# Last eight blocks of a row-mean laid out so that a partition ends with sixteen neighbouring rows, stored as 128 runs of 64 B

## Chip, cores and metric

One core of one Trainium2 chip. The metric is the device time of one execution in microseconds; the median of several executions is quoted.

The *span* runs from the program's first instruction to its last one. The *time* is longer by what is called *outside* below. SyncE *issues* the transfers; the issue is the time that it spends on handing one over. Each load raises a semaphore by 16, in single counts (the records of the kernel before have 176 for eleven loads); a store is waited for at 16 too, in fewer records for the small ones (5 for the last store of the kernel before). The *landing* of a transfer is when its last count arrives.

## The reference

```python
x = np.random.randn(64, 256, 8192).astype(np.float32)   # 512 MiB

def reference(x):
    return np.mean(x, axis=2)                             # (64, 256) float32
```

That is 16384 rows of 8192 numbers, each row one mean.

## The kernel before

The 16384 rows are 64 blocks of 256 rows: 128 partitions (`P`) times two rows (`R`). Loads of 8 MiB go through three slots; VectorE sums them. The last block comes in shrinking pieces, shared between VectorE and ScalarE, so that little work is left when the last byte lands.

```python
    NB = N // (P * R)          # 64 blocks
    LB = NB - 1                # the last block is treated apart
    x_v = x_f[0 : LB * P * R].rearrange("(p n r) s -> n p r s", p=P, r=R)
    x_l = x_f[LB * P * R : N].rearrange("(r p) s -> r p s", p=P)
    out_bulk = o_f[0 : LB * P * R].rearrange("(p n) -> p n", p=P)
    out_last = o_f[LB * P * R : N].rearrange("(r q j) -> r q j", q=P // SQ, j=SQ)
    # ... cut ...
    def store_last(r):         # a column of 128 sums -> 4 rows of 32 sums -> 4 runs of 128 B
        nc.vector.transpose(out=fin_t[r][:], in_=fin[r][:])
        return nc.sync.dma_start(out=out_last[r], in_=fin_t[r][0:P:SQ, :])
    # ... 63 loads and sums, the chunks of the last block: cut ...
    nc.vector.tensor_scalar_mul(out=bulk[:], in0=res[:], scalar1=inv)
    nc.sync.dma_start(out=out_bulk, in_=bulk[:])
    scaled_sum(fin[0][:, 0:1], head[:])
    st = store_last(0)
    # ... cut ...
    untracked(scaled_sum(fin[1][:, 0:1], fin_in[:, 0 : lastw + k]))._wait_ge(sem, 16)
    with tc.issue_after(st.ins):
        last_store = store_last(1)
```

In the bulk each partition owns 126 neighbouring rows of HBM, so partitions lie 4032 KiB apart. In the last block neighbouring rows lie in neighbouring partitions, and each column of 128 sums must be turned before it can be stored in long runs. The kernel also writes its own exit. There GpSimd clears the semaphores and then waits for the last store:

```python
    with nc.body("clears", parent=parent, valid_engines=[POOL]):
        nc.gpsimd.sem_clear(range(used[0], stored))
        nc.gpsimd.wait_ge(last_sem, 16).then_inc(last_sem, -16)
```

Of the kernel before, what the change touches and what calls it, by code (L numbers as in the profile page):

```python
# [8 lines left out]
SLOTS = 3  # L9
LOAD_SEMS = 6  # L10
FETCH_BLOCK = 128
LAST_CHUNKS = (4096, 2048, 1024, 512, 256, 256)

ACT_FROM = 512
SQ = 32


@with_exitstack
def kernel(
# [5 lines left out]
    nc = tc.nc  # L25
    P = nc.NUM_PARTITIONS
    F32 = mybir.dt.float32
# [4 lines left out]
    B, C, S = x.shape  # L32
    N = B * C
    R = ROWS
    assert R == 2 and N % (P * R) == 0, (N, P, R)
    NB = N // (P * R)
    LB = NB - 1
    assert SLOTS <= LB and sum(LAST_CHUNKS) == S
    inv = 1.0 / float(S)
    half = S // 2  # L40

    x_f = x.rearrange("b c s -> (b c) s")
    o_f = out.rearrange("b c -> (b c)")

    x_v = x_f[0 : LB * P * R].rearrange("(p n r) s -> n p r s", p=P, r=R)
    x_l = x_f[LB * P * R : N].rearrange("(r p) s -> r p s", p=P)
    out_bulk = o_f[0 : LB * P * R].rearrange("(p n) -> p n", p=P)
    out_last = o_f[LB * P * R : N].rearrange("(r q j) -> r q j", q=P // SQ, j=SQ)

    pool = ctx.enter_context(tc.tile_pool(name="sb", bufs=1))  # L50
    slots = [nc.alloc_sbuf_tensor(f"xt{i}", [P, R, S], F32) for i in range(SLOTS)]
    load_sem = [tc.alloc_semaphore(f"load{i}") for i in range(LOAD_SEMS)]
    tail_sem = [tc.alloc_semaphore(f"tail{i}") for i in range(len(LAST_CHUNKS) + 1)]

    res = pool.tile([P, LB * R], F32)
    bulk = pool.tile([P, LB * R], F32)
    fin = [pool.tile([P, SQ], F32, name=f"fin{r}") for r in range(R)]
    fin_t = [pool.tile([P, SQ], F32, name=f"fin_t{r}") for r in range(R)]
    for r in range(R):
        nc.vector.memset(fin[r][:], 0.0)  # L60



# [1 line left out]
    def untracked(ins):  # L65
        tc.declare_no_dep(ins.ins, group="loads", reason="own semaphores")
        return ins

    def load(dst, src, sem):
        ld = untracked(nc.sync.dma_start(out=dst, in_=src))  # L70
        tc.add_to_no_dep_group("loads", ld.ins)
        tc.no_tile_sem_insts.add(ld.ins.name)
        ld.then_inc(sem, 16)
        return ld

    def loaded(n, ins):
        ins._wait_ge(load_sem[n % LOAD_SEMS], 16 * (n // LOAD_SEMS + 1))

    def dve_sum(dst, src):
        return untracked(nc.vector.tensor_reduce(out=dst, in_=src, axis=X, op=ADD))  # L80

    def act_sum(dst, src):
        return untracked(nc.scalar.activation(out=src, in_=src, func=COPY, accum_out=dst))  # L83

    def scaled_sum(dst, src):
        return nc.vector.tensor_scalar(  # L86
            out=src,
            in0=src,
            scalar1=inv,
            scalar2=None,  # L90
            op0=mybir.AluOpType.mult,
            op1=ADD,
            accum_out=dst,
        )

    def store_last(r):
        nc.vector.transpose(out=fin_t[r][:], in_=fin[r][:])  # L97
        return nc.sync.dma_start(out=out_last[r], in_=fin_t[r][0:P:SQ, :])

    for n in range(LB):  # L100
        xt = slots[n % SLOTS]
        ld = load(xt[:], x_v[n], load_sem[n % LOAD_SEMS])
        if n == 0:
            first = ld
        if n < LB - 1:
            loaded(n, dve_sum(res[:, n * R : (n + 1) * R], xt[:]))
        else:
            loaded(n, dve_sum(res[:, n * R : n * R + 1], xt[:, 0, :]))
            loaded(n, act_sum(res[:, n * R + 1 : n * R + 2], xt[:, 1, :]))

    nparts = 2 * len(LAST_CHUNKS)
    lastw = LAST_CHUNKS[-1]
    xl = slots[LB % SLOTS]
    fin_in = nc.alloc_sbuf_tensor("fin_in", [P, lastw + nparts], F32)
    head = pool.tile([P, 2], F32)

    ld = load(xl[:, 0, :], x_l[0], tail_sem[0])
    dve_sum(head[:, 0:1], xl[:, 0, 0:half])._wait_ge(tail_sem[0], 16)
    act_sum(head[:, 1:2], xl[:, 0, half:S])._wait_ge(tail_sem[0], 16)

    pos, k = 0, 0
    for c, w in enumerate(LAST_CHUNKS):
        last = c == len(LAST_CHUNKS) - 1
        dst = fin_in[:, 0:w] if last else xl[:, 1, pos : pos + w]
        sem = tail_sem[c + 1]
        with tc.issue_after(ld.ins):
            ld = load(dst, x_l[1, :, pos : pos + w], sem)
        if not last:
            wv = w // 2 if w >= ACT_FROM else w
            part = fin_in[:, lastw + k : lastw + k + 2]  # L130
            dve_sum(part[:, 0:1], xl[:, 1, pos : pos + wv])._wait_ge(sem, 16)
            k += 1
            if wv < w:
                act_sum(part[:, 1:2], xl[:, 1, pos + wv : pos + w])._wait_ge(sem, 16)
                k += 1
        pos += w

    nc.vector.tensor_scalar_mul(out=bulk[:], in0=res[:], scalar1=inv)  # L138
    nc.sync.dma_start(out=out_bulk, in_=bulk[:])

    scaled_sum(fin[0][:, 0:1], head[:])
    st = store_last(0)

    with tc.issue_after(st.ins):
        st = nc.sync.wait_ge(tail_sem[-2], 16)
    with tc.issue_after(st.ins):
        st = nc.sync.addr_align(FETCH_BLOCK, offset=0, max_nops=0)
    untracked(scaled_sum(fin[1][:, 0:1], fin_in[:, 0 : lastw + k]))._wait_ge(sem, 16)
    with tc.issue_after(st.ins):
        last_store = store_last(1)  # L150



# [18 lines left out]
    end_bb, parent = blocks[2], nc.bb_map[body_bb.name]  # L172
# [3 lines left out]
    with nc.body("scratch", parent=parent, valid_engines=[DVE]):  # L176
# [15 lines left out]
        name=nc.get_next_instruction_name(), engine=DVE, associate_branch=over.name  # L192
# [12 lines left out]
    POOL, SP = mybir.EngineType.Pool, mybir.EngineType.SP  # L205
    exit_ins = list(end_bb.instructions)
    sems = {w.id: (w.ant_name, w.wait_value) for w in exit_ins[0].sync_info.on_wait}
    assert exit_ins[0].engine == SP and isinstance(exit_ins[0], mybir.InstDrain)
    stored = last_store.ins.sync_info.on_update[0].id
    used = sorted({*sems, *(s.num for s in (*load_sem, *tail_sem))})  # L210
    assert used == list(range(used[0], stored + 1))
    with nc.body("awaits", parent=parent, valid_engines=[SP]):
        for num, (name, count) in sems.items():
            if num != stored:
                nc.sync.wait_ge(bass.SemaphoreHandle(name, num), count)
    last_sem = bass.SemaphoreHandle(*sems[stored][:1], stored)
    with nc.body("clears", parent=parent, valid_engines=[POOL]):
        nc.gpsimd.sem_clear(range(used[0], stored))
        nc.gpsimd.wait_ge(last_sem, 16).then_inc(last_sem, -16)
    made = {b.name: b for b in blocks}  # L220
    blocks.remove(made["awaits"])
    blocks.remove(made["clears"])
    reports = [
        i
        for i in exit_ins[1 : exit_ins.index(next(i for i in exit_ins if i.engine == POOL))]
        if isinstance(i, mybir.InstDrain)
    ]
    drain, gather = [i for i in exit_ins if i.engine == POOL][:2]
    end_bb.instructions = [
        *made["awaits"].instructions, *reports, drain, gather, *made["clears"].instructions  # L230
    ]
# [30 lines left out]
```

## Time and profile before

| | before |
|---|---|
| time, median of 3 runs (lowest to highest) | 1245.99 us (1245.82 to 1245.99) |
| time and span of the profiled run | 1246.58 and 1244.67 us |
| busy: DMA queue, VectorE | 99.8%, 87% |
| period of the 8 MiB loads in the steady part | 19.35 us |

How to read it: the row of DMA digits in the page gives the queue's busy tenths in 40 slices, the waits tell who waited for whom, and the order in time of the last microseconds shows what follows the last byte. The lines themselves are in the prediction below. The profiled run is 0.6 us above the median.

### The profile page before, as it was taken

To read this page: it belongs to the slowest core of one execution; us is meant where nothing else is said; L and a number is where in the kernel's file an instruction comes from. 1 tells how busy PE (TensorE), PEld (TensorE's weight loads), DVE (VectorE), ACT (ScalarE), POOL (GpSimd) and SP (SyncE) were. 2 spreads that over 40 slices of the span, in tenths; PEclk is the share of its full clock that TensorE was granted. 3 is DMA by queue.
4 is the path that set the end of the run, shared out by engine and by line. 5 is a ranking of instruction groups with operands and counts; after the bars stand their busy time and mean duration, and the time that the engine had idled before them with its cause. 6 is when DMAs were issued, how large, how long until landed. Compare 5 with 4: busy or idle time off the path is not lost.

```text
span 1244.7 us, 199 instructions
## 1 busy us (share of the span) xinstructions
DVE 1087.0 (87%) x78; ACT 16.5 (1%) x13; POOL 0.2 (0%) x4
## 2 busy tenths in 40 slices
DVE  2898988989889889898898988989889898898988
ACT  0000000000000000000000000000000000000004
POOL 0000000000000000000000000000000000000000
DMA  9999999999999999999999999999999999999998
GB/s 434 411 436 438 438 438 436 428 417 438 438 438 438 436 432 413 438 438 438 438 436 438 411 434 438 438 438 438 436 425 419 438 438 438 438 436 434 411 438 373
DMA packets 10241, 536.95 MB, mean 431 GB/s; under 512 B 1280, under 2 KB 1536, under 8 KB 1792
## 3 DMA queue, kind: packets, MB, share of 16 engines
q1 hardware_dynamic: 10240, 536.94, 99.8%
q14 instruction: 1, 0.01, 0.0%
HBM read 536.87 MB, written 0.07 MB: 431 GB/s over the span
## 4 chain that ended last, share of the span: by engine, by line
DMA 70%; DVE 29%; SPq 0%; issue 0%; DVEq 0%
DMA xt<-in_x_dram 70%; DVE res L80 29%; DVE fin_in L80 0%; SPq L70 0%; DVE fin_in L86 0%; DVE fin_t L97 0%; DVEq L86 0%
## 5 line engine op out<-in xcount | busy, mean ns | idle before, releaser
L80 DVE TENSOR_REDUCE res<-xt 128x2 f32<-128x16384 f32 (+1 forms) x63 | 1076.3, 17084 | 153.8 <-DMA xt<-in_x_dram 153.8
L83 ACT ACT_TABLE_LOAD x1 | 1.3, 1283 | 1181.6 <-DVE res L80 1181.6
L83 ACT ACTIVATE xt<-xt 128x8192 f32<-128x8192 f32 (+5 forms) x6 | 14.7, 2443 | 43.9 <-DMA xt<-in_x_dram 43.7
L80 DVE TENSOR_REDUCE fin_in<-xt 128x1 f32<-128x256 f32 (+3 forms) x5 | 4.9, 1005 | 0.3 <-DMA xt<-in_x_dram 0.2
L80 DVE TENSOR_REDUCE head<-xt 128x1 f32<-128x4096 f32 x1 | 4.4, 4420 | 0.7 <-DMA xt<-in_x_dram 0.7
L83 ACT ACTIVATION_READ_ACCUMULATOR xt<-xt 128x1 f32 x6 | 1.1, 186 | 0.0
L60 DVE MEMSET fin<- 128x32 f32 x2 | 0.1, 85 | 0.9 <-PEq L246 0.9
L86 DVE TENSOR_SCALAR_CACHE_REDUCE fin_in<-fin_in 128x265 f32<-128x265 f32 x1 | 0.4, 431 | 0.2 <-DVE fin_in L80 0.2
L97 DVE STREAM_TRANSPOSE fin_t<-fin 128x32 f32<-128x32 f32 x2 | 0.4, 212 | 0.1
L138 DVE TENSOR_SCALAR bulk<-res 128x126 f32<-128x126 f32 x1 | 0.2, 228 | 0.1
L86 DVE TENSOR_SCALAR_CACHE_REDUCE head<-head 128x2 f32<-128x2 f32 x1 | 0.2, 155 | 0.1
L246 POOL MEMSET const-bfloat16-1.0<- 128x1 bf16 x1 | 0.1, 101 | 0.0
L246 POOL MEMSET const-uint8-127<- 128x1 uint8 x1 | 0.1, 101 | 0.0
L246 POOL MEMSET const-float32-0.0<- 128x1 f32 x1 | 0.1, 98 | 0.2 <-issue 0.2
L246 POOL MEMSET const-float32-1.0<- 128x1 f32 x1 | 0.1, 98 | 0.0
L86 DVE DVE_READ_ACCUMULATOR fin_in<-fin_in 128x1 f32 x1 | 0.1, 84 | 0.0
L86 DVE DVE_READ_ACCUMULATOR head<-head 128x1 f32 x1 | 0.1, 83 | 0.0
## 6 DMA issues: line engine op xcount, KB each, us to landing
xt<-in_x_dram SPq DMA_DIRECT2D x1, 4096.0 KB, 31.1
xt<-in_x_dram SPq DMA_DIRECT2D x1, 2048.0 KB, 35.7
xt<-in_x_dram SPq DMA_DIRECT2D x1, 1024.0 KB, 37.7
xt<-in_x_dram SPq DMA_DIRECT2D x63, 40.8
xt<-in_x_dram SPq DMA_DIRECT2D x1, 512.0 KB, 38.5
xt<-in_x_dram SPq DMA_DIRECT2D x1, 256.0 KB, 38.7
xt<-in_x_dram SPq DMA_DIRECT2D x1, 128.0 KB, 38.6
fin_in<-in_x_dram SPq DMA_DIRECT2D x1, 128.0 KB, 38.5
```

The source lines that it names most:

```text
L60: nc.vector.memset(fin[r][:], 0.0)
L80: return untracked(nc.vector.tensor_reduce(out=dst, in_=src, axis=X, op=ADD))
L83: return untracked(nc.scalar.activation(out=src, in_=src, func=COPY, accum_out=dst))
L86: return nc.vector.tensor_scalar(out=src, in0=src, scalar1=inv, scalar2=None, op0=mybir.AluOpType.mult, op1=ADD, accum_out=dst,)
L97: nc.vector.transpose(out=fin_t[r][:], in_=fin[r][:])
L138: nc.vector.tensor_scalar_mul(out=bulk[:], in0=res[:], scalar1=inv)
L246: nc = _bacc.Bacc("TRN2", target_bir_lowering=False, num_devices=1)
```

## The change

Intent: the last eight blocks are laid out so that every partition holds 16 neighbouring rows of HBM. Their sums then already stand as a run of 64 B per partition and need no transpose; one store of 128 such runs takes the place of a transpose and a store of 4 runs of 128 B. The first 56 blocks become contiguous 8 MiB each, and their sums are turned early, on TensorE, while loads run.

```diff
+RUN = 16
-    x_v = x_f[0 : LB * P * R].rearrange("(p n r) s -> n p r s", p=P, r=R)
-    x_l = x_f[LB * P * R : N].rearrange("(r p) s -> r p s", p=P)
-    out_bulk = o_f[0 : LB * P * R].rearrange("(p n) -> p n", p=P)
-    out_last = o_f[LB * P * R : N].rearrange("(r q j) -> r q j", q=P // SQ, j=SQ)
+    TB = NB - RUN // R
+    x_v = x_f[0 : TB * P * R].rearrange("(n p r) s -> n p r s", p=P, r=R)
+    x_t = x_f[TB * P * R : N].rearrange("(p n r) s -> n p r s", p=P, r=R)
+    out_bulk = o_f[0 : TB * P * R].rearrange("(n p r) -> n p r", p=P, r=R)
+    out_tail = o_f[TB * P * R : N].rearrange("(p t) -> p t", t=RUN)
     ... (identity on GpSimd, other tiles: cut)
-    nc.vector.tensor_scalar_mul(out=bulk[:], in0=res[:], scalar1=inv)
-    nc.sync.dma_start(out=out_bulk, in_=bulk[:])
-    scaled_sum(fin[0][:, 0:1], head[:])
-    st = store_last(0)
+    bulk = pool.tile([P, P, R], F32)
+    for r in range(R):
+        ps = psum_pool.tile([P, P], F32, name=f"ps{r}")
+        nc.tensor.transpose(out=ps[:TB, :], in_=res[:, r, :], identity=ident[:])
+        nc.vector.tensor_scalar_mul(out=bulk[:TB, :, r], in0=ps[:TB, :], scalar1=inv)
+    st = nc.sync.dma_start(out=out_bulk, in_=bulk[:TB])
+    nc.vector.tensor_scalar_mul(out=tail_out[:, 0 : RUN - R], in0=tail[:], scalar1=inv)
+    scaled_sum(tail_out[:, RUN - R : RUN - 1], head[:])
     ...
-    untracked(scaled_sum(fin[1][:, 0:1], fin_in[:, 0 : lastw + k]))._wait_ge(sem, 16)
+    untracked(scaled_sum(tail_out[:, RUN - 1 : RUN], fin_in[:, 0 : lastw + k]))._wait_ge(sem, 16)
-        last_store = store_last(1)
+        last_store = nc.sync.dma_start(out=out_tail, in_=tail_out[:])
     ... (exit)
-    with nc.body("clears", parent=parent, valid_engines=[POOL]):
-        nc.gpsimd.sem_clear(range(used[0], stored))
-        nc.gpsimd.wait_ge(last_sem, 16).then_inc(last_sem, -16)
+    with nc.body("clears", parent=parent, valid_engines=[SP, POOL]):
+        ... (GpSimd clears the others, in runs)
+        for eng, num in zip((nc.sync,), stored):
+            sem = bass.SemaphoreHandle(sems[num][0], num)
+            eng.wait_ge(sem, 16).then_inc(sem, -16)
```

More of the change, by code (lines that the diff above doesn't have):

```diff
@@ L14 @@
 ACT_FROM = 512
-SQ = 32
+RUN = 16
 @with_exitstack
@@ L37 @@
     LB = NB - 1
-    assert SLOTS <= LB and sum(LAST_CHUNKS) == S
+    TB = NB - RUN // R
+    assert SLOTS <= TB <= P and sum(LAST_CHUNKS) == S
     inv = 1.0 / float(S)
@@ L43 @@
     o_f = out.rearrange("b c -> (b c)")
-    x_v = x_f[0 : LB * P * R].rearrange("(p n r) s -> n p r s", p=P, r=R)
-    x_l = x_f[LB * P * R : N].rearrange("(r p) s -> r p s", p=P)
-    out_bulk = o_f[0 : LB * P * R].rearrange("(p n) -> p n", p=P)
-    out_last = o_f[LB * P * R : N].rearrange("(r q j) -> r q j", q=P // SQ, j=SQ)
+    x_v = x_f[0 : TB * P * R].rearrange("(n p r) s -> n p r s", p=P, r=R)
+    x_t = x_f[TB * P * R : N].rearrange("(p n r) s -> n p r s", p=P, r=R)
+    out_bulk = o_f[0 : TB * P * R].rearrange("(n p r) -> n p r", p=P, r=R)
+    out_tail = o_f[TB * P * R : N].rearrange("(p t) -> p t", t=RUN)
     pool = ctx.enter_context(tc.tile_pool(name="sb", bufs=1))
+    psum_pool = ctx.enter_context(
+        tc.tile_pool(name="psum", bufs=1, space=bass.MemoryType.PSUM)
+    )
     slots = [nc.alloc_sbuf_tensor(f"xt{i}", [P, R, S], F32) for i in range(SLOTS)]
@@ L53 @@
     tail_sem = [tc.alloc_semaphore(f"tail{i}") for i in range(len(LAST_CHUNKS) + 1)]
-    res = pool.tile([P, LB * R], F32)
-    bulk = pool.tile([P, LB * R], F32)
-    fin = [pool.tile([P, SQ], F32, name=f"fin{r}") for r in range(R)]
-    fin_t = [pool.tile([P, SQ], F32, name=f"fin_t{r}") for r in range(R)]
-    for r in range(R):
-        nc.vector.memset(fin[r][:], 0.0)
+    res = pool.tile([P, R, TB], F32)
+    tail = pool.tile([P, RUN - R], F32)
+    tail_out = pool.tile([P, RUN], F32)
+    ident = pool.tile([P, P], F32)
+    nc.gpsimd.memset(ident[:], 0.0)
+    nc.gpsimd.affine_select(
+        out=ident[:],
+        in_=ident[:],
+        compare_op=mybir.AluOpType.not_equal,
+        fill=1.0,
+        base=0,
+        pattern=[[-1, P]],
+        channel_multiplier=1,
+    )
     def untracked(ins):
@@ L94, in scaled_sum @@
         )
-    def store_last(r):
-        nc.vector.transpose(out=fin_t[r][:], in_=fin[r][:])
-        return nc.sync.dma_start(out=out_last[r], in_=fin_t[r][0:P:SQ, :])
     for n in range(LB):
         xt = slots[n % SLOTS]
-        ld = load(xt[:], x_v[n], load_sem[n % LOAD_SEMS])
+        src = x_v[n] if n < TB else x_t[n - TB]
+        ld = load(xt[:], src, load_sem[n % LOAD_SEMS])
         if n == 0:
             first = ld
-        if n < LB - 1:
-            loaded(n, dve_sum(res[:, n * R : (n + 1) * R], xt[:]))
-        else:
-            loaded(n, dve_sum(res[:, n * R : n * R + 1], xt[:, 0, :]))
-            loaded(n, act_sum(res[:, n * R + 1 : n * R + 2], xt[:, 1, :]))
+        k = (n - TB) * R
+        if n < TB:
+            loaded(n, dve_sum(res[:, :, n], xt[:]))
+        elif n < LB - 1:
+            loaded(n, dve_sum(tail[:, k : k + R], xt[:]))
+        else:
+            loaded(n, dve_sum(tail[:, k : k + 1], xt[:, 0, :]))
+            loaded(n, act_sum(tail[:, k + 1 : k + R], xt[:, 1, :]))
     nparts = 2 * len(LAST_CHUNKS)
@@ L115 @@
     head = pool.tile([P, 2], F32)
-    ld = load(xl[:, 0, :], x_l[0], tail_sem[0])
+    x_l = x_t[LB - TB]
+    ld = load(xl[:, 0, :], x_l[:, 0, :], tail_sem[0])
     dve_sum(head[:, 0:1], xl[:, 0, 0:half])._wait_ge(tail_sem[0], 16)
@@ L126 @@
         with tc.issue_after(ld.ins):
-            ld = load(dst, x_l[1, :, pos : pos + w], sem)
+            ld = load(dst, x_l[:, 1, pos : pos + w], sem)
         if not last:
@@ L208 @@
     assert exit_ins[0].engine == SP and isinstance(exit_ins[0], mybir.InstDrain)
-    stored = last_store.ins.sync_info.on_update[0].id
+    stored = [st.ins.sync_info.on_update[0].id for st in (last_store,)]
     used = sorted({*sems, *(s.num for s in (*load_sem, *tail_sem))})
-    assert used == list(range(used[0], stored + 1))
     with nc.body("awaits", parent=parent, valid_engines=[SP]):
         for num, (name, count) in sems.items():
-            if num != stored:
+            if num not in stored:
                 nc.sync.wait_ge(bass.SemaphoreHandle(name, num), count)
-    last_sem = bass.SemaphoreHandle(*sems[stored][:1], stored)
-    with nc.body("clears", parent=parent, valid_engines=[POOL]):
-        nc.gpsimd.sem_clear(range(used[0], stored))
-        nc.gpsimd.wait_ge(last_sem, 16).then_inc(last_sem, -16)
+    with nc.body("clears", parent=parent, valid_engines=[SP, POOL]):
+        rest = [n for n in range(used[0], used[-1] + 1) if n not in stored]
+        while rest:
+            run = [n for k, n in enumerate(rest) if n == rest[0] + k]
+            nc.gpsimd.sem_clear(range(run[0], run[-1] + 1))
+            rest = rest[len(run) :]
+        for eng, num in zip((nc.sync,), stored):
+            sem = bass.SemaphoreHandle(sems[num][0], num)
+            eng.wait_ge(sem, 16).then_inc(sem, -16)
     made = {b.name: b for b in blocks}
@@ L222 @@
     blocks.remove(made["clears"])
+    drain, gather = [i for i in exit_ins if i.engine == POOL][:2]
     reports = [
-        i
-        for i in exit_ins[1 : exit_ins.index(next(i for i in exit_ins if i.engine == POOL))]
-        if isinstance(i, mybir.InstDrain)
+        i for i in exit_ins[1 : exit_ins.index(drain)] if isinstance(i, mybir.InstDrain)
     ]
-    drain, gather = [i for i in exit_ins if i.engine == POOL][:2]
     end_bb.instructions = [
```

## The prediction

> **What bounds the kernel now.** I read the page first (busy shares, the slices, the DMA queue), then the waits of VectorE and of the SyncE queue, then the chain that ended last and the order in time of the last 15 us. From the page:
>
> ```profile
> DVE 1087.0 (87%) x78; ACT 16.5 (1%) x13; POOL 0.2 (0%) x4
> ...
> DMA  9999999999999999999999999999999999999998
> ...
> q1 hardware_dynamic: 10240, 536.94, 99.8%
> ```
>
> The 16 DMA engines are full in every slice and busy for 99.8% of the span; VectorE, the busiest compute engine, has 13% left. So bytes divided by DMA rate set the time. The waits say the same from the other side:
>
> ```profile
> DVE res L80 <- DMA xt<-in_x_dram: 153.8, 63, 21.2
> ```
>
> ```profile
> SPq L70 <- DVE res L80: 1178.7, 61, 37.9
> ```
>
> VectorE waits for data before each of 63 sums (21.2 us once for the first load, some 2.1 us each later). SyncE waits for VectorE too, but that wait is harmless: with three slots one whole load is always queued behind the one in flight. The chain of waits shows the rhythm:
>
> ```profile
> 1142.89 40.78 DMA xt<-in_x_dram
> 1183.67 0.02 issue
> 1183.70 17.23 DVE res L80
> ```
>
> A load lands 40.78 us after its issue, that is 2 x 19.35 us of transfer (its own and the one ahead of it) plus some 2 us. The page's chain says "DMA 70%, DVE 29%", but the 17 us sums on it are only what the queue's depth covers; nothing would shorten if they did. In the semaphore records load follows load every 19.35 us from the sixth on (8 MiB / 19.35 us = 434 GB/s), and in the packet records nearly every 64 KiB packet takes 2.418 to 2.426 us. Only the first load (22.2 us) and the third to fifth (+0.16, +0.16, +0.07 us) are off that beat.
>
> What is not bandwidth is the very end. The order in time:
>
> ```profile
> 1239.49 2.73 DVE L80 TENSOR_REDUCE fin_in<-xt 128x1 f32<-128x1024 f32 x4 [0.21 <-DMA xt<-in_x_dram]
> ...
> 1242.37 0.43 DVE L86 TENSOR_SCALAR_CACHE_REDUCE fin_in<-fin_in 128x265 f32<-128x265 f32 x1 [0.15 <-DVE fin_in L80]
> 1242.72 0.08 DVE L86 DVE_READ_ACCUMULATOR fin_in<-fin_in 128x1 f32 x1
> 1242.84 0.21 DVE L97 STREAM_TRANSPOSE fin_t<-fin 128x32 f32<-128x32 f32 x1
> 1243.08 0.52 SPq L98 DMA_DIRECT2D out_dram<-fin_t  x1
> ```
>
> The last sums shrink with the chunks, so only 1.0 us pass from the last semaphore count of the last chunk (1242.20) through the closing scaled sum and the transpose to the store's issue at 1243.08. The store's last count arrives at 1244.63 (semaphore records) and the span ends at 1244.67. So the store, issue to landing, costs 1.55 us, and the kernel ends on it. The span's 1244.7 stands against 1246.58 us measured for the same run: 1.9 us lie outside the program and stay.
>
> [...]the 4-row store leaves four late increments (1244.56 to 1244.63) after one early one (1244.08), and its issue is long, 0.52 and 0.64 us against 0.33 to 0.43 us for loads on 16. [...]Here 504 B packets took 28 ns and 128 B ones 11 ns, so the trace shows no large penalty per packet; no run has 64 B yet. [...]before has no 512 KiB pitch (bulk pitch 4032 KiB, last block 32 KiB), so its trace is silent. [...]
>
> **The change, part by part.**
> 1. First 56 loads: partition pitch 4032 KiB becomes 64 KiB, one contiguous 8 MiB. Packets stay 64 KiB, 128 per load. The packets already run at one constant time, so the engines bind and not the addresses: 0. At most the 0.39 us of the third to fifth load could vanish.
> 2. Last eight blocks: each partition reads its 16 neighbouring rows, pitch 512 KiB. [...]
> 3. The small last chunks (4096 down to 256 columns) also get the 512 KiB pitch: 128 pieces of 1 KiB each a power of two apart. They took 46 ns each before. [...]
> 4. Two TensorE transposes and two scaled copies from PSUM now stand on VectorE after the 56th sum. [...]2 x 0.23 us (the old 126-column scaling took 0.228)[...], with a whole load in reserve behind it. Cost 0. The identity is made by GpSimd during the first load. Cost 0.
> 5. The bulk store, 56 rows of 1 KiB, is issued at some 1204 us, right behind the last loads, instead of 1231.46. It shares their queue, so it still moves after them, as the old one did (its packets ran from 1240.9 to 1241.8, last count 1242.37). Cost 0.
> 6. The first small store (issued 1237.11, 0.64 us) and its transpose go. Both lay beside loads. Gain 0.
> 7. The last transpose goes: from the count at 1242.82 to the issue at 1243.08 is 0.26 us; the wait of SyncE still costs 0.02. Gain 0.24 us.
> 8. The last store is 128 pieces of 64 B on 16 engines instead of 4 of 128 B on 4. Issue 0.35 to 0.40 instead of 0.52: gain 0.13. Against it: eight packets per engine rather than one, 7 x some 12 ns = 0.1 us; and the slowest of 16 engines counts. On the idle queue of the first load, engines took up their first packets from 1.02 to 1.54 us after the issue, and in every load one engine's count comes 0.38 to 0.48 us after the other fifteen. The four engines of the old store lay within 0.07 us. I take 0.4 us. Sum: +0.37, and issue to landing becomes about 1.55 + 0.37 = 1.9 us.
> 9. SyncE rather than GpSimd waits for the last count; the other clears were done before it (GpSimd's at 1244.43). 0, give or take 0.1.
>
> Sum of 7 and 8: 1242.84 + 1.92 = 1244.76 for the last count, 0.13 us later than before. [...]
>
> **The rivals.**
> A, the store as meant: if the lag of one engine belongs to a busy queue only, the eight short packets cost 0.1 us and the shorter issue pays for them; then 0.24 us are gained, and with the early hiccup gone as well 0.6: 1245.4 to 1245.8. For it: the 128 B packets took only 11 ns. Against it: the 0.39 us lag is there in the very first load, on an idle queue.
> B, the 512 KiB pitch bites: [...] For it: [...]a DMA queue with no slack at all, so every slower packet is paid in full. Against it: 4032 KiB was no trouble[...].
> C, VectorE's new wait for TensorE delays the release of a slot. It would have to last over 19 us to empty the queue. I give it no weight.
>
> **Range and chances.** Without B (some 60%) I expect 1245.4 to 1246.6[...]. Predicted 1246.5, eight in ten between 1245.3 and 1250.5. Two per cent are 25 us; the whole tail after the last byte is 2.5 us, so nothing here can gain 25, and a loss of 25 needs the pitch to cost 16% over 155 us. Faster 0.01, same 0.97, slower 0.02.
>
> **What would show it.** Item 1: sums of the first 56 blocks still every 19.35 us. Items 2 and 3: the starts of the last eight sums and the landing of the chunks; a beat over 19.4 us, or packets above 2.43 us, is rival B. Item 4: VectorE idle for under 2.1 us before the 57th sum, as before any other. Items 7 and 8: no transpose in the chain, the store issued 0.02 us after the closing sum, its last count 1.8 to 2.1 us later; some 1.5 us would be rival A. I am wrong if the beat changes in the first 56 loads, or if 64 B pieces take much longer than 12 ns each.

The sum came to 1245.99 + 0.13 + 0.5 = 1246.6 us, told as 1246.5: -0.24 us for item 7, +0.37 for item 8, and 0.4 and 0.1 for the 512 KiB pitch in items 2 and 3.

## The result, and the profile after

| | before | after |
|---|---|---|
| time, median of 6 runs (lowest to highest) | 1245.95 us (1245.82 to 1246.13) | 1245.12 us (1244.88 to 1245.31) |
| profiled run: time, span | 1246.58, 1244.67 us | 1245.31, 1243.94 us |
| time minus span of the profiled run | 1.91 us | 1.37 us |

The ratio is 0.9993, with a 95% interval of 0.9980 to 1.0006. At the 2% that counts as a difference the two kernels are the same. Still, no run of one kernel lies among the runs of the other, and the time lies 0.18 us under the range of the prediction, which ended at 1245.3. The prediction expected 0.5 us more than before; 0.8 us less came.

The page of the changed kernel, busy shares and DMA queue:

```profile
PE 0.6 (0%) x2; PEld 0.2 (0%) x2; DVE 1087.1 (87%) x76; ACT 16.5 (1%) x13; POOL 0.7 (0%) x6
...
q1 hardware_dynamic: 10294, 536.94, 99.9%
```

Nothing of the bound has moved. Its waits of VectorE (what waited, on what, total, times, longest):

```profile
DVE res L92 <- DMA xt<-in_x_dram: 139.4, 56, 21.9
...
DVE tail L92 <- DMA xt<-in_x_dram: 13.8, 7, 2.1
...
DVE bulk L155 <- PE ps L154: 0.6, 1, 0.6
```

The longest wait is the one for the first load, 21.9 us here and 21.2 before; there two memsets kept VectorE busy up to 1.0 us, from where its wait counts, so this does not show a slower load. The wait for TensorE is 0.6 us, once. The order in time around the 57th sum shows what became of it:

```profile
1103.91 0.60 PE L154 MATMUL ps<-ident,res 128*56 128x128 f32 x2 [1103.91 <-DVE res L92]
1104.33 0.50 DVE L155 TENSOR_SCALAR bulk<-ps 56x128 f32<-56x128 f32 x2 [0.57 <-PE ps L154]
1105.90 17.22 DVE L92 TENSOR_REDUCE tail<-xt 128x2 f32<-128x16384 f32 x1 [1.07 <-DMA xt<-in_x_dram]
```

After both copies VectorE still waits 1.07 us for the load. The end, in order of time:

```profile
1239.10 2.76 DVE L92 TENSOR_REDUCE fin_in<-xt 128x1 f32<-128x1024 f32 x4 [0.20 <-DMA xt<-in_x_dram]
...
1242.01 0.43 DVE L98 TENSOR_SCALAR_CACHE_REDUCE fin_in<-fin_in 128x265 f32<-128x265 f32 x1 [0.15 <-DVE fin_in L92]
1242.37 0.08 DVE L98 DVE_READ_ACCUMULATOR fin_in<-fin_in 128x1 f32 x1
1242.48 0.36 SPq L167 DMA_DIRECT2D out_dram<-tail_out  x1
```

The transpose is gone and the store follows the closing sum at once. The page of the DMA issues gives its landing:

```profile
out_dram<-tail_out SPq DMA_DIRECT2D x1, 8.0 KB, 1.4
```

I split both profiled runs at the same events (semaphore records; "store" is the last one, its end is the end of the span):

| piece, us | before | after | difference |
|---|---|---|---|
| start to the landing of the first load | 22.23 | 21.85 | -0.38 |
| from there to the landing of the last chunk but one | 1219.55 | 1219.57 | +0.02 |
| from there to the issue of the last store (VectorE) | 1.31 | 1.06 | -0.25 |
| store, issue to the end of the span | 1.59 | 1.47 | -0.12 |
| end of the span to the end of the time | 1.91 | 1.37 | -0.54 |
| sum | 1246.58 | 1245.31 | -1.27 |

The sum is -1.27 us, though the medians differ by 0.83. Part of it is thus peculiar to the pair of runs that happened to be profiled. Even the +0.02 of the second row is chance: both executions had some 0.4 us of late loads on the way (three loads in the one, two that came after 19.65 and 19.45 us in the other), while of the other profiles, pitch_4M apart, all but one have 1219.13 to 1219.42 us there. Two theories on the first row and two on the last one had to be told apart.

That the last row lies behind the span, and not before its start, is in the semaphore records: the last count of the closing comes 2.03 us after the span's end before and 1.49 us after it now, 0.54 us apart.

### The profile page after: what moved, and what is told of

Its sections match the earlier page's. It is cut to its first block, busy times and chain, and to the rows that moved or that the text cites. A ratio compares the mean times of both kernels' runs of the same rounds, so it can differ in the third digit from the quotient of the medians. Undisturbed runs are those within 1.5% of the kernel's fastest.

```text
span 1243.9 us, 206 instructions
## 1 busy us (share of the span) xinstructions
PE 0.6 (0%) x2; PEld 0.2 (0%) x2; DVE 1087.1 (87%) x76; ACT 16.5 (1%) x13; POOL 0.7 (0%) x6
## 4 chain that ended last, share of the span: by engine, by line
DMA 70%; DVE 29%; issue 0%; SPq 0%; DVEq 0%
DMA xt<-in_x_dram 70%; DVE res L92 26%; DVE tail L92 3%; DVE fin_in L92 0%; SPq L82 0%; DVEq L173 0%; DVE fin_in L98 0%; DVEq L98 0%
## 5 line engine op out<-in xcount | busy, mean ns | idle before, releaser
L92 DVE TENSOR_REDUCE res<-xt 128x2 f32<-128x16384 f32 x56 | 964.4, 17222 | 139.4 <-DMA xt<-in_x_dram 139.4
L92 DVE TENSOR_REDUCE tail<-xt 128x2 f32<-128x16384 f32 (+1 forms) x7 | 112.0, 16001 | 13.8 <-DMA xt<-in_x_dram 13.8
```

The lines of the kernel that those rows point to most:

```text
L92: return untracked(nc.vector.tensor_reduce(out=dst, in_=src, axis=X, op=ADD))
```

## Experiments

Each kernel was timed in five rounds beside the kernel before, whose medians in the three groups were 1245.99, 1245.95 and 1246.04 us. "Outside" is time minus span, averaged over all runs of a kernel; with spans recorded to 0.1 us it scattered by no more than 0.06 us around its mean in any kernel, and for the kernel before it was 1.90 to 1.92 in each group.

### bulk_contig: the bulk loads alone

Kernel before, the output order wrong:

```diff
-    x_v = x_f[0 : LB * P * R].rearrange("(p n r) s -> n p r s", p=P, r=R)
+    x_v = x_f[0 : LB * P * R].rearrange("(n p r) s -> n p r s", p=P, r=R)
```

> The kernel before with one line changed: the first 63 loads read one contiguous 8 MiB each (pitch 64 KiB per partition instead of 4032 KiB); everything else, the transposes and the last store too, stays. The output rows come in the wrong order on purpose. Theory L (the layout of the first load decides how late the slowest DMA engine takes up its stream, and that lag is carried to the end): the first load lands at 21.85 us as in the changed kernel, instead of 22.23; from the second load on no engine lags 0.4 us; time 0.4 us shorter, about 1245.55. Theory S (the lag belongs to something else in the changed program, such as the identity on GpSimd or other code, or to chance): first load at 22.2, time as before, 1245.95.

Measured: 1246.03 us (1245.94 to 1246.62) against 1245.99; outside 1.91. Its profile has the first load at 21.91 us, yet the time does not differ from the kernel before. So theory L falls for this pair of pitches: going from 4032 KiB to contiguous loads gains nothing in the median. The -0.38 us of the table is no part of the change's gain. The late engine belongs to an execution and not to a layout: in three profiles with the very same loads the last count of a load came 0.38 to 0.48 us after the other fifteen (kernel before), 0.16 to 0.31 us (before_sp) and at most 0.04 us (store_k16). Nor do the 22.23 us alone explain why the first profile ran 0.6 us over its median: its early loads lost another 0.39 us, and before_sp, with its first load at 22.25 us, ended its span 0.39 us sooner.

### tail_only, tail_only_again and tail_pitch4032: the tail alone

Changed kernel, the bulk put back to rows that lie together in a partition, without TensorE:

```diff
-    x_v = x_f[0 : TB * P * R].rearrange("(n p r) s -> n p r s", p=P, r=R)
+    x_v = x_f[0 : TB * P * R].rearrange("(p n r) s -> n p r s", p=P, r=R)
     ... (out_bulk, res and bulk as in the kernel before, identity and transposes out)
```

> The changed kernel with its first 56 loads put back to a large pitch (now 112 rows of a partition together, 3584 KiB) and its bulk store to one of 128 x 448 B, without TensorE; the last eight blocks and the last store of 64 B pieces stay. Theory L: the first load lands at some 22.2 us again, the end keeps its gain (transpose 0.25, store 0.12), time about 1245.55. Theory S: first load at 21.85, time about 1245.15.

> The tail_only kernel once more, on another occasion. If its 0.4 us over the changed kernel belong to its pitch of 3584 KiB: 1245.45 again and the first load at 22.3 or more. If they were chance: 1245.1 and 21.9 to 22.1.

tail_pitch4032 differs from it only in taking its 56 blocks from the old 63-block layout (output wrong):

```diff
-    x_v = x_f[0 : TB * P * R].rearrange("(p n r) s -> n p r s", p=P, r=R)
+    x_v = x_f[0 : LB * P * R].rearrange("(p n r) s -> n p r s", p=P, r=R)
```

> The tail_only kernel, but its 56 bulk loads at the pitch of the kernel before, 4032 KiB, instead of 3584 KiB (output wrong on purpose). tail_only was 0.4 us slower than the changed kernel, with engines taking up their first packets between 1.0 and 2.1 us instead of 1.0 and 1.7. If the pitch of 3584 KiB did that: 1245.1 here, first load at 21.9 to 22.0. If it is chance from run to run or belongs to the missing TensorE part: 1245.45 again.

Measured: 1245.44 us (1245.37 to 1245.59), again 1245.38 (1245.23 to 1245.83), and with 4032 KiB 1245.14 (1244.84 to 1245.61). For tail_only theory L had 1245.55 and theory S 1245.15, and neither counted the exit, whose part was not known yet. What came lies nearer to L, but not for L's reason: with 4032 KiB the tail alone is as fast as the whole change. The two profiles at 3584 KiB have the first load at 22.38 and 22.19 us and engines that start their first packet as late as 2.1 and 2.5 us; the one at 4032 KiB has 22.11 (21.9 to 22.0 was expected) and 1.5. But store_k16 and bulk_contig, at 4032 KiB and with contiguous loads, had their last engine start at 2.05 and 2.02 us, so late starts are not peculiar to 3584 KiB. The waits of VectorE in the second profile at 3584 KiB:

```profile
DVE res L78 <- DMA xt<-in_x_dram: 139.4, 56, 22.2
```

So the pitch of 3584 KiB may cost some 0.3 us: two groups of five runs against one, on different chips and with overlapping ranges. This is not shown, and a cause is open. What matters for the change: with the bulk at 4032 KiB its whole gain is there (1245.14 us), so it sits in the tail and the exit and none of it in the bulk layout.

### after_again

The changed kernel without an edit.

> The changed kernel as it is, on the same chip as the others. Both theories: about 0.8 us under the kernel before, 1245.1; first load at 21.85; last store 1.43 us from issue to its last count.

Measured: 1245.04 us (1244.82 to 1245.49), first load at 21.96, store 1.46 us from issue to the end of the span, outside 1.35. The gain repeats: 0.95 us here.

### before_sp, after_pool, after_act: who waits last

The kernel before, waiting with SyncE:

```diff
-    with nc.body("clears", parent=parent, valid_engines=[POOL]):
+    with nc.body("clears", parent=parent, valid_engines=[SP, POOL]):
         nc.gpsimd.sem_clear(range(used[0], stored))
-        nc.gpsimd.wait_ge(last_sem, 16).then_inc(last_sem, -16)
+        nc.sync.wait_ge(last_sem, 16).then_inc(last_sem, -16)
```

> The kernel before, with one thing changed: SyncE instead of GpSimd waits for the last store's count at the very end. Loads, transposes and stores stay. Theory W (the engine that ends last sets how long the closing after the program takes: so far 1.91 us past the span's end where GpSimd waited, 1.37 us where SyncE did): span as before, time minus span 1.37, time about 0.54 us shorter, 1245.45. Theory P (the 0.54 us between the two groups comes from something else in the changed program, such as TensorE being used or the short waits): time minus span stays 1.9 and the time 1246.0.

The changed kernel, waiting with GpSimd, and in another run with ScalarE (there `valid_engines` of this block names ScalarE too):

```diff
-        for eng, num in zip((nc.sync,), stored):
+        for eng, num in zip((nc.gpsimd,), stored):     # after_act: (nc.scalar,)
```

> The changed kernel with the last wait given back to GpSimd, all else as changed. Theory W: time minus span 1.91, time 0.54 us longer than the changed kernel, about 1245.65, so 0.35 us under the kernel before, which is then what the transpose and the store are worth. Theory P: 1.37 and 1245.1.

> The changed kernel with ScalarE as the engine that waits for the last count. If theory W holds[...], the time past the span's end changes again: between 1.1 and 1.9 us, and the time between 1244.8 and 1245.7. Under theory P it stays at 1.37 and 1245.1.

| kernel | last wait on | time, us (lowest to highest) | span of the median run, us | outside, us |
|---|---|---|---|---|
| before, same rounds | GpSimd | 1245.95 (1245.88 to 1246.13) | 1244.0 | 1.90 |
| before_sp | SyncE | 1245.81 (1245.68 to 1245.86) | 1244.2 | 1.60 |
| after_pool | GpSimd | 1245.66 (1245.49 to 1246.36) | 1243.7 | 1.92 |
| after_act | ScalarE | 1245.30 (1245.18 to 1245.48) | 1243.8 | 1.55 |
| after_again (other rounds) | SyncE | 1245.04 (1244.82 to 1245.49) | 1243.7 | 1.35 |

after_pool decides between the theories. With nothing changed but the waiting engine, 0.57 us of the time outside the span come back (1.92 against 1.35) while the span stays at 1243.7. Theory W holds and P falls.

before_sp gives only part of it, 0.30 us, and its profile offers a reason. After its last store of 4 runs SyncE sits in a drain for 0.31 us (0.007 us in the changed kernel) before it lets GpSimd go on, and GpSimd ends its clearing only 0.29 us before the end of the span, against 0.65 us in the changed kernel. If the closing after the program takes 1.91 us counted from GpSimd's last instruction and 1.37 us counted from SyncE's, whichever ends later, then before_sp must show 1.91 - 0.29 = 1.62 us; it shows 1.60. For the changed kernel GpSimd would allow 1.91 - 0.65 = 1.26, so SyncE's 1.37 holds; since that is the figure that was put in, only before_sp tests this rule. The time of before_sp fell by only 0.14 us since its spans came out 0.1 to 0.2 us longer; its profile has the first load at 22.25 us, and whether that is chance I did not test.

### store_4B, run8, store_k16: the pieces of the last store

The kernel before without its transposes, each column stored as it is (and its exit written as in the changed kernel, with GpSimd waiting):

```diff
-    out_last = o_f[LB * P * R : N].rearrange("(r q j) -> r q j", q=P // SQ, j=SQ)
+    out_last = o_f[LB * P * R : N].rearrange("(r q j) -> r q j", q=P, j=1)
-        nc.vector.transpose(out=fin_t[r][:], in_=fin[r][:])
-        return nc.sync.dma_start(out=out_last[r], in_=fin_t[r][0:P:SQ, :])
+        return nc.sync.dma_start(out=out_last[r], in_=fin[r][:, 0:1])
     ... (exit: cut)
```

> The kernel before with its two transposes taken away: each last column of 128 sums is stored as 128 pieces of 4 B on 16 engines. If the cost of the last store lies in its issue and flight and not in its pieces: transpose 0.24 gone, store 1.43 instead of 1.55, together 0.36 us shorter, about 1245.6, with 4 B packets of about 10 ns. If small pieces do cost[...], 4 B pieces show it: packets well over 12 ns and a store of over 1.6 us; then time 1245.8 or more. First load at 22.2 under theory L.

Measured: 1251.25 us (1251.04 to 1251.61), over 5 us slower than the kernel before. The DMA issues of this kernel (bytes, median time to landing):

```profile
out_dram<-bulk SPq DMA_DIRECT2D x1, 63.0 KB, 15.2
out_dram<-fin SPq DMA_DIRECT2D x2, 0.5 KB, 8.6
```

The waits of SyncE's queue show that it had to wait in the exit even for the bulk store, which ran beside the first of the two stores (the last store landed later still, and ended the kernel):

```profile
SPq L212 <- DMA out_dram<-bulk: 3.5, 1, 3.5
```

The last store took 6.7 us from issue to its last count, against 1.43 us for 128 runs of 64 B. The packet records hardly show it: the 4 B packets took 7 to 9 ns each, and all but nine were through 1.0 us after the issue, those nine (one engine's share, by their number) 2.2 us after it. The counts come later, spread over 3.5 us. My expectation looked for the penalty in the packets and would have missed it. The 6.7 us are not those of one such store alone: the counts of the first one went on to 1246.79 us, 4.4 us past the issue of the second. What a single store of 128 runs of 4 B costs was not tried. A column stored straight needs neither transpose nor layout; two of them cost over 5 us here.

The changed kernel with shorter runs:

```diff
-RUN = 16
+RUN = 8
```

> The changed kernel with 8 neighbouring rows per partition instead of 16, so the last store has 128 pieces of 32 B. The 4 B pieces took 6.7 us from issue to landing against 1.43 for 64 B. [...] If there is no such cost at 32 B: 1.46 us from issue to end and 1245.1.

Measured: 1245.08 us (1244.94 to 1245.57), store 1.45 us to the end of the span, landing 1.4 us in its DMA issues:

```profile
out_dram<-tail_out SPq DMA_DIRECT2D x1, 4.0 KB, 1.4
```

Runs of 32 B cost no more than 64 B (1.47 and 1.46 us in the two profiles of the changed kernel); the trouble of the 4 B runs was not there yet.

The kernel before with each small store over 16 partitions instead of 4 (wrong order):

```diff
-    out_last = o_f[LB * P * R : N].rearrange("(r q j) -> r q j", q=P // SQ, j=SQ)
+    out_last = o_f[LB * P * R : N].rearrange("(r q j) -> r q j", q=16, j=P // 16)
-        return nc.sync.dma_start(out=out_last[r], in_=fin_t[r][0:P:SQ, :])
+        return nc.sync.dma_start(out=out_last[r], in_=fin_t[r][0 : P : P // 16, 0 : P // 16])
```

> The kernel before with its transposes and GpSimd's last wait kept, but each small store spread over 16 partitions (16 pieces of 32 B on 16 engines, wrong order on purpose) instead of 4 pieces of 128 B on 4 engines. If the store's gain of 0.12 us in the changed kernel comes from using all 16 engines (shorter issue): issue 0.33 to 0.36 instead of 0.52 us, issue to span's end some 1.40 to 1.47 instead of 1.59, SyncE's drain after it about 0.01 to 0.05 instead of 0.31 to 0.38 us, time 1245.85. If it comes from the pieces or the missing transpose: issue 0.52 and 1.59 stay. Small pieces of 32 B may cost by themselves, as the 4 B pieces did: then issue to end over 1.6.

Measured: 1246.11 us (1246.03 to 1246.34). In the order in time the issue is as long as ever:

```profile
1242.44 0.51 SPq L98 DMA_DIRECT2D out_dram<-fin_t  x1
```

All 16 engines took part (16 separate counts, 1243.92 to 1244.08), and still the issue took 0.51 us and the store 1.68 us to the end of the span. So the number of engines, to which I had put down the long issue, is not its reason. The third branch of the expectation, over 1.6 us, came out as well; but run8 stores pieces of 32 B in 1.45 us, so their size is not the reason. The last stores with a short issue (0.33 to 0.36 us) all take all 128 partitions one after another; those with a long one take every 32nd or every 8th partition. Number and step were not told apart on purpose, but the bulk stores give a hint: issued while loads were running, those of 56 and 60 partitions in a row (changed kernel and run8) took 0.46 and 0.48 us, one of 128 (tail_only) 0.43. Fewer partitions in a row thus add little, which points to the step; it stays open.

### pitch_4M: the pitch rival at its sharpest

The changed kernel's last seven 8 MiB loads have a pitch of 512 KiB. They came every 19.351 us, as the loads before them did (19.351 in the median), so rival B of the prediction did not occur. To see whether a pitch can slow the loads at all, the kernel before was given exactly 4096 KiB (output wrong):

```diff
-    x_v = x_f[0 : LB * P * R].rearrange("(p n r) s -> n p r s", p=P, r=R)
+    x_v = x_f.rearrange("(p n r) s -> n p r s", p=P, r=R)
```

> The kernel before with its bulk loads at a pitch of exactly 4096 KiB per partition instead of 4032 KiB (output wrong on purpose). [...] If loads in 64 KiB pieces are held by the engines: 19.35 us and 1246.0.

Measured: 1617.16 us (1556.52 to 1711.52). The profile comes from a run of 1618.85 us, with the clock at 1.000; the gap to 1246 us is far beyond the scatter of either kernel. Its page:

```profile
DVE 1086.9 (67%) x78; ACT 16.4 (1%) x13; POOL 0.2 (0%) x4
...
DMA  9999999999999999999999999999999999999997
GB/s 285 311 308 289 311 310 311 295 302 306 308 311 305 310 308 318 308 311 311 336 336 310 336 306 340 342 347 350 358 340 370 373 373 370 384 386 391 400 409 308
```

This is a good lesson in reading: the DMA digits are as full as before and the queue is busy 98.9%, but the rate has fallen from 438 to some 310 GB/s in the first half, to climb back to some 400 near the end; why it climbs is open. Here busy engines were not fast engines. The 64 KiB packets took 3.16 us in the median, 2.42 before.

## Why the prediction was wrong

The parts that were to decide it were named, but the sizes of three were wrong. The sum had +0.63 us in all (told as 0.5): 0.5 us of it for a pitch that cost nothing, +0.37 for a store that gained 0.12, and 0 for an exit that gained 0.54. These three make up 1.53 us and turn +0.63 into -0.90; -0.83 was measured. The step that failed in kind is "1.9 us lie outside the program and stay".

- **Item 1 (bulk loads, 0):** right for these pitches: bulk_contig moved the median by 0.04 us (at 4096 KiB it would not have been, 1617 us). Theory L, made after the result, again read the late engine of one profiled execution as a property of the kernel.
- **Items 2 and 3 (512 KiB pitch, 0.5 us):** wrong by being there at all; no trace of this case stood behind them. With some 60% given to no loss, the median case is no loss, so 0.4 us could not be a median. The beat of the last seven loads was 19.351 us, the 64 KiB packets took 2.42 us in the median in both profiles, and the 1 KiB packets 46 and 47 ns.
- **Item 4 (TensorE and copies in VectorE's gap, 0):** right; 0.57 us of waiting and 0.50 us of copies, with 1.07 us to spare. The two transposes (of fp32) took 0.39 and 0.42 us, 0.60 us together since they overlap.
- **Items 5 and 6 (bulk store early, first small store gone, 0):** in keeping with the profile, where no exit wait on a bulk store appears; not tried alone.
- **Item 7 (transpose, -0.24):** right. The stretch from the last chunk but one to the issue is 1.31 us in all five profiled kernels with the transpose and 1.06 us in all nine without it. (From the count at 1242.20 to the issue 0.88 us pass and not the 1.0 that the prediction read; the sum does not use it.)
- **Item 8 (store, +0.37):** mis-sized, measured -0.12 us (1.59 to 1.47; 1.44 to 1.47 in all kernels that store 32 or 64 B per partition). The shorter issue came (0.361 us, -0.16). From the issue's end to the last count it took 1.07 us instead of 1.03: against the 0.5 us that were added for eight packets per engine and for the lag of one engine, 0.04 came. The 64 B packets took 11 ns in the median, and the sixteen counts of the last store arrived within 0.18 us. The 0.4 us of lag were taken from the loads of one profiled execution; in the changed kernel's own profile the loads have next to none of it (0.01 us in the median). In tail_pitch4032 they have 0.25 us, and the store's counts still lie within 0.18 us. The short issue was not a matter of 16 engines instead of 4 either, as store_k16 showed (0.51 us on 16).
- **Item 9 (SyncE waits instead of GpSimd, 0 give or take 0.1):** mis-sized, measured -0.54 us, the largest term of all. I had written that the 1.9 us outside the program "stay". They depend on which engine ends last, as after_pool showed by changing that alone.

The parts that were shown add up to -0.25 - 0.12 - 0.54 = -0.91 us, against -0.83 and -0.95 us in the two measurements of the change. Rival A, the store as meant, had the tail right (0.24 us gained and the store no longer). That its 1245.4 came near 1245.12 is luck: it rests on an early hiccup that was not the change's to remove, and lacks item 9.

What comes after the span is in the semaphore records of the two profiles: one semaphore counts up in two chains, mostly in steps of 0.02 to 0.05 us, and from 0.75 to 1.41 us after the span's end (0.26 to 0.91 us in the changed kernel) nearly every other semaphore has one record; all of it ends 2.03 us after the span's end before and 1.49 us after it in the changed kernel. In the kernel before, where GpSimd ends last, the first count of the chain comes 0.56 us after the span's end. In the changed kernel, where SyncE does, two counts have come already, and the next one follows 0.14 us after the span's end. That the chain waits there for the engine that ends last is my reading of these times and was not shown.

No experiment pointed to a version clearly faster than the changed kernel: runs of 32 B are equal (1245.08), ScalarE as the last waiter is slower (1245.30).

## What to carry to other kernels

When a kernel is bound by its loads to 99.8%, as here, a change that leaves their rate as it is (19.35 us per 8 MiB) is left with the two ends, and the ends include what comes after the last instruction (1.91 us before, 1.37 us after): compare time minus span, run by run, before explaining a difference inside. One profiled execution is one draw; a start that came 0.4 us late in it is not a property of the kernel until a second run shows it. Results that stand as one column did best here when the row layout gathered them into runs of 32 B or 64 B per partition (1.45 and 1.47 us from the store's issue to the end of the span), while two stores of 4 B runs cost over 5 us and a transpose 0.25 us.
